# Latent attention with v stationary, P moving in two column halves of the array, and P divided by its sums while it is turned

## The chip, the cores and the metric

One core of one Trainium2 chip runs the whole program. The metric is the device time of one execution in microseconds (us); the median of three runs of the kernel before is 2729.82 us. PE is TensorE, PEld its loads of stationary operands ("weights"), DVE is VectorE, ACT is ScalarE, POOL is GpSimd, SP is SyncE.

## What is computed

Two sequences (512 and 256 tokens, 1024 features, all float32) go through two layers of a gated encoder with four branches and a convolutional feed-forward part. The change touches one branch, the latent attention with four heads. Its core, cut from the reference:

```python
q = rms_norm(q, g_qn); k = rms_norm(k, g_kn)      # heads of 64 + 32 (rope) values
q = q * (dqk ** -0.5)
def block(qi):                                     # 128 queries at a time
    s = jnp.einsum('bqhd,bkhd->bhqk', qi, k, preferred_element_type=jnp.float32)
    p = jax.nn.softmax(s, axis=-1)                 # over all keys of the sequence
    return jnp.einsum('bhqk,bkhd->bqhd', p.astype(v.dtype), v)   # v: 64 per head
...
return o @ w_o
```

The result of a 128-token tile is 128 tokens by 4 x 64 values. What follows (the product with `w_o`) wants it turned, with the 256 features on the partitions and split into a high and a low part.

## The kernel before

The code issues instructions in the order in which it calls them; each engine works through its own queue in that order, and waits between engines follow from the tiles. Two kinds of work are laced together. The large projections (`tm`, matmuls at L522, and `fm`, L498) run in a straight line, and after each step they call `q`, which advances a planned time `now` and then lets pending generators (`fast`, `slow`) issue their next piece when their planned time has come. Where the main line needs a generator's results it calls `drain`, which runs it to its end with nothing of the main line in between.

`mla` is such a generator. It starts under the projection of the first dilated group (`dil_proj(0)`); `self.drain(ed)` behind that projection then runs the rest of it alone. After the projections of latent q, k and v it has q and k turned per head (`qkT`, 96 partitions), and v as tokens by 256 features, 64 for each head. Then it makes a list of jobs, one for each tile of 128 queries and each head: 4 tiles x 4 heads with 4 key blocks (512 keys), then 2 tiles x 4 heads with 2 key blocks, 24 jobs a layer. A job is a tuple of steps:

- `score` (PE, L904): the 128 x S scores, S = 512 or 256, in a PSUM tile
- `low` (DVE, L909): the row minimum (the scores have their sign turned)
- `expo` (ACT, L915): the exponent into `P`, and in the same instruction the row sums, read out by an ACTIVATION_READ_ACCUMULATOR
- `turn` (PE, L921 calling `tr`, L511): each 128x128 block of P is transposed into PSUM; `tr` is TensorE's transpose, with the identity as second operand
- `copy` (DVE L930 for even heads, ACT L928 for odd ones): PSUM to `PT`
- `value` (PE, L937): for each key block a matmul with the turned P as stationary operand and the head's 64 columns of v moving; the four heads of a tile fill 256 columns of one PSUM tile `po`
- `done` (after the fourth head): DVE takes the reciprocals of the four sums (L944) and multiplies `po` by them into `mo` (L946); a generator put into `fast` then transposes `mo` in two blocks (`to_bin`, L511) and splits each into high and low (`split`: ACT L481, DVE L482).

`pipe` (L764) issues the steps of neighbouring jobs in turn. In its iteration i it calls, in three groups with a third of `w` planned time between them: score of job i and `done` of an earlier job; low of i and turn of i - 1; expo of i, copy of i - 1 and value of i - 2. PSUM tiles of this kind (`ps`) come from four buffers, SBUF tiles `s` (P, PT) from seven, small `st` tiles from eight. An f32 matmul is one instruction in the program and leaves two records in the trace (two weight loads, two passes); a transpose leaves one.

## Time and profile before

| | |
|---|---|
| runs | 2726.26, 2729.82, 2730.07 us; median 2729.82 |
| the profiled execution | 2730.13 us, span of its trace 2728.4 us |
| PE busy / PEld / DVE / ACT / POOL | 98% / 89% / 63% / 42% / 23% of the span |
| the chain that ended last | PE 86%, DVE 8%, issue 2%, ACT 2% |
| instructions of `value` (L937), both layers | 320 records, 42.2 us busy, loads 40.4 us |
| instructions of `score` (L904), both layers | 96 records, 44.8 us busy |

In the page a matmul's duration includes its way through the array, so busy times of pipelined matmuls overlap; what one costs is the distance between starts. In the timeline, neighbours of one line are merged (x8), and a bracket gives the engine's idle time ahead of the row and what ended it. PEclk is the share of TensorE's full clock that was granted (1.00 is 2.4 GHz, 0.50 is 1.2 GHz).

### The profile page before, as it was taken

To read this page: it belongs to the slowest core of one execution; us is meant where nothing else is said; L and a number is where in the kernel's file an instruction comes from. 1 tells how busy PE (TensorE), PEld (TensorE's weight loads), DVE (VectorE), ACT (ScalarE), POOL (GpSimd) and SP (SyncE) were. 2 spreads that over 40 slices of the span, in tenths; PEclk is the share of its full clock that TensorE was granted. 3 is DMA by queue.
4 is the path that set the end of the run, shared out by engine and by line. 5 is a ranking of instruction groups with operands and counts; after the bars stand their busy time and mean duration, and the time that the engine had idled before them with its cause. 6 is when DMAs were issued, how large, how long until landed. Compare 5 with 4: busy or idle time off the path is not lost.

```text
span 2728.4 us, 40139 instructions
## 1 busy us (share of the span) xinstructions
PE 2677.2 (98%) x15196; PEld 2439.2 (89%) x15196; DVE 1729.2 (63%) x3048; ACT 1141.3 (42%) x2333; POOL 634.0 (23%) x592
## 2 busy tenths in 40 slices
PE   9999999999998999999999999999999989999999
PEld 8779998888898899999987799988888989999998
DVE  6644448887437866686746454478873388766875
ACT  6443443223224554554544434432232255544553
POOL 3402123122222212222314021131121212222221
PEclk9999999999999999999999999999999999999999
DMA  5101113212232466646731111131212325567556
GB/s 167 43 28 37 41 56 114 63 62 62 62 129 81 107 148 128 155 121 147 193 94 43 28 40 48 51 114 63 66 59 62 132 74 127 137 130 161 125 136 163
DMA packets 143264, 258.87 MB, mean 95 GB/s; under 512 B 20192, under 2 KB 36192, under 8 KB 143072
## 3 DMA queue, kind: packets, MB, share of 16 engines
q1 hardware_dynamic: 118368, 197.59, 22.7%
q0 software_dynamic: 24704, 58.73, 12.4%
q8 instruction: 119, 1.95, 0.3%
q14 instruction: 73, 0.60, 0.1%
HBM read 205.78 MB, written 48.91 MB: 93 GB/s over the span
## 4 chain that ended last, share of the span: by engine, by line
PE 86%; DVE 8%; issue 2%; ACT 2%; POOL 1%; DMA 1%; SPq 0%; DVEq 0%; ACTq 0%; POOLq 0%
PE mm L498 35%; PE ps L498 26%; PE mm L522 16%; PE ps L511 3%; DVE wlo L453 2%; PE ps L904 1%; PE ps L1137 1%; PE ps L937 1%; PE ps L1088 1%; DMA raw<-wu 1%; PE ps L1140 1%; POOL st L529 1%; DVE b L612 1%; DVE hl L628 0%; PE ps L851 0%
## 5 line engine op out<-in xcount | busy, mean ns | idle before, releaser
L453 DVE TENSOR_TENSOR wlo<-raw,whi 128x512 fp32r<-128x512 f32 (+1 forms) x616 | 480.8, 790 | 142.3 <-ACT whi L444 117.9
L498 PE MATMUL ps<-b,whi 128*128 128x384 f32 (+2 forms) x1888 | 466.2, 340 | 17.3 <-ACT s L1532 11.7
L444 ACT CAST whi<-raw 128x512 fp32r<-128x512 f32 (+1 forms) x616 | 370.0, 614 | 237.2 <-PE ps L498 72.3
L498 PEld LDWEIGHTS ps<-b,whi 128*128 128x128 f32 x1888 | 329.7, 191 | 34.4 <-ACT s L1532 12.3
L498 PE MATMUL mm<-b,whi 128*128 128x512 f32 (+1 forms) x1504 | 322.9, 336 | 0.6 <-DVE b L1576 0.6
L522 PE MATMUL mm<-whi,hh 128*128 128x512 f32 (+2 forms) x752 | 308.8, 411 | 7.5 <-ACT hh L547 5.7
L498 PE MATMUL mm<-hh,whi 128*128 128x512 f32 (+1 forms) x1152 | 302.1, 343 | 0.0
L498 PE MATMUL ps<-b,wlo 128*128 128x384 f32 (+2 forms) x944 | 299.1, 339 | 0.0
L498 PE MATMUL mm<-hh,wlo 128*128 128x512 f32 (+1 forms) x1152 | 296.8, 338 | 0.0
L498 PE MATMUL mm<-hl,whi 128*128 128x512 f32 (+1 forms) x1152 | 294.7, 337 | 0.0
L522 PE MATMUL mm<-whi,hl 128*128 128x512 f32 (+2 forms) x752 | 278.8, 371 | 0.8 <-DVE hl L554 0.8
L522 PE MATMUL mm<-wlo,hh 128*128 128x512 f32 (+2 forms) x752 | 278.5, 370 | 0.0
L498 PE MATMUL ps<-hh,whi 128*128 128x384 f32 x768 | 259.6, 338 | 8.5 <-ACT whi L444 8.5
L498 PEld LDWEIGHTS mm<-b,whi 128*128 128x128 f32 x1504 | 237.0, 188 | 26.6 <-DVE b L1576 1.2
L498 PE MATMUL ps<-hl,whi 128*128 128x384 f32 x768 | 259.4, 338 | 1.2 <-DVE hl L628 1.2
L498 PE MATMUL ps<-hh,wlo 128*128 128x384 f32 x768 | 258.2, 336 | 0.0
L529 POOL TENSOR_TENSOR st<-st,mhalf 128x16 f32<-128x16 f32 (+5 forms) x50 | 95.0, 1900 | 573.6 <-DVE st L1012 355.7
L1368 POOL TENSOR_TENSOR b<-b,b 128x768 f32<-128x768 f32 x48 | 100.2, 2087 | 463.4 <-DVE b L1363 463.4
L498 PEld LDWEIGHTS mm<-hh,whi 128*128 128x128 f32 x1152 | 177.3, 189 | 26.6 <-issue 3.1
L522 PEld LDWEIGHTS mm<-whi,hh 128*128 128x128 f32 x752 | 177.6, 236 | 25.6 <-issue 10.2
L498 PEld LDWEIGHTS mm<-hl,whi 128*128 128x128 f32 x1152 | 175.7, 188 | 25.1
L498 PEld LDWEIGHTS mm<-hh,wlo 128*128 128x128 f32 x1152 | 176.0, 188 | 24.4
(233 smaller groups left out, 4607.9 us busy)
## 6 DMA issues: line engine op xcount, KB each, us to landing
raw<-wu SPq DMA_DIRECT2D x600, 256.0 KB, 2.7
xsp<-y POOLq DMA_DIRECT2D x66, 384.0 KB, 5.8
raw<-wu POOLq DMA_DIRECT2D x80, 256.0 KB, 4.9
b<-xsp SPq DMA_DIRECT2D x24, 384.0 KB, 6.8
xsp<-b POOLq DMA_DIRECT2D x22, 384.0 KB, 5.7
do<-ot SPq DMA_DIRECT2D x36, 132.0 KB, 1.8
b<-do SPq DMA_DIRECT2D x12, 384.0 KB, 3.5
raw<-wu SPq DMA_DIRECT2D x16, 208.0 KB, 3.6
```

The source lines that it names most:

```text
L444: self.nc.scalar.copy(hi, raw)
L453: self.nc.vector.tensor_sub(lo, raw, hi.bitcast(F32))
L498: nc.tensor.matmul(ap, w, x[:, c0:c1], start=(k == 0 and i == 0 and not more), stop=(k == K - 1 and i == 2), skip_group_check=more)
L511: self.nc.tensor.transpose(out, x, self.ident)
L522: nc.tensor.matmul(ap, x[:, cols], w, start=(k == 0 and i == 0), stop=(k == 7 and i == 2))
L529: self.nc.gpsimd.tensor_tensor(r, ms, self.mhalf[:, 0:n], op=ALU.pow)
L612: nc.vector.scalar_tensor_tensor(h, h, g[:, k:k + 1], self.rbc[:, cols], op0=ALU.mult, op1=ALU.mult)
L904: nc.tensor.matmul(sc[:, 0:S], qkT[hh][:, 128 * t:128 * t + 128], qkT[4 + hh][:, 128 * t0:128 * t0 + S], start=True, stop=True)
L937: nc.tensor.matmul(sh["po"][:, hh, :], PT[:, 128 * kb:128 * kb + 128], v[(t0 + kb) // 3][:, (t0 + kb) % 3, 64 * hh:64 * hh + 64], start=(k ...
L1088: nc.tensor.matmul(sc[:, x, y, 0:W], qT[y][rr, 128 * t:128 * t + 128], kT[y][rr, k0:k0 + W], start=True, stop=True)
L1137: nc.tensor.matmul(po[:, 0, 2 * y + par, :], PT[0:c - a, 2 * z + y, :], vv[:, hc], start=(z == 0), stop=(z == 1))
L1368: nc.gpsimd.tensor_add(a, a, t)
```

## The change

`turn` no longer calls the transpose. A new step `diag` takes the reciprocal of the head's sums, and multiplies the identity by it, row by row; `turn` is then an ordinary matmul with a block of P stationary and that diagonal moving, which turns the block and divides it at once. `value` has v stationary (128 keys x 64 features) and the turned P moving (128 queries); it is called for every head but acts for odd ones alone, and then for two heads, key block by key block in alternation. The even head's result goes to PSUM partitions 0 to 63, the odd one's to 64 to 127, so the two take different column halves of the array and `po` comes out with features on the partitions. `done` therefore has nothing to transpose or to multiply: it splits the two halves of `po`, in line and no longer from a generator. `pipe` calls `diag` (step 7) at the start of the iteration after `expo`, ahead of `done`; the condition on `len(jobs[j])` leaves the other attention, whose jobs have seven steps, as it was.

```diff
-            for group in (((0, 0), (6, 2)), ((1, 0), (3, 1)), ((2, 0), (4, 1), (5, 2))):
+            for group in (((0, 0), (7, 1), (6, 2)), ((1, 0), (3, 1)), ((2, 0), (4, 1), (5, 2))):
...
-                    if 0 <= j < n:
+                    if 0 <= j < n and f < len(jobs[j]):
...
         def expo():
             e["P"] = P = self.s(S)
-            if hh == 0:
-                sh["l"] = self.st(4)
-            nc.scalar.activation(P, e.pop("sc")[:, 0:S], AF.Exp, bias=e["mn"], scale=-1.0,
-                                 accum_out=sh["l"][:, hh:hh + 1])
+            e["l"] = self.st(1)
+            nc.scalar.activation(P, e.pop("sc")[:, 0:S], AF.Exp, bias=e["mn"], scale=-1.0, accum_out=e["l"])
+
+        def diag():
+            r = self.st(1)
+            nc.vector.reciprocal(r, e.pop("l"))
+            e["dg"] = dg = self.pm.tile([128, 128], F32, tag="mo", name=self.nm("mo"), bufs=2)
+            nc.vector.tensor_scalar_mul(dg, self.ident, r)
 
         def turn():
-            P = e.pop("P")
+
+            P, dg = e.pop("P"), e.pop("dg")
             e["pt"] = pt = self.ps()
             for kb in range(n):
-                self.tr(pt[:, 128 * kb:128 * kb + 128], P[:, 128 * kb:128 * kb + 128])
+                nc.tensor.matmul(pt[:, 128 * kb:128 * kb + 128], P[:, 128 * kb:128 * kb + 128], dg, start=True,
+                                 stop=True)
...
         def value():
-            if hh == 0:
-                sh["po"] = self.ps((128, 4, 64))
-            PT = e.pop("PT")
+
+            if hh % 2 == 0:
+                return
+            if hh == 1:
+                sh["po"] = self.ps((128, 2, 128))
+            PT = [sh.pop(hh - 1), sh.pop(hh)]
             for kb in range(n):
-                nc.tensor.matmul(sh["po"][:, hh, :], PT[:, 128 * kb:128 * kb + 128],
-                                 v[(t0 + kb) // 3][:, (t0 + kb) % 3, 64 * hh:64 * hh + 64], start=(kb == 0),
-                                 stop=(kb == n - 1))
+                for x in range(2):
+                    h = hh - 1 + x
+                    nc.tensor.matmul(sh["po"][64 * x:64 * x + 64, hh // 2, :],
+                                     v[(t0 + kb) // 3][:, (t0 + kb) % 3, 64 * h:64 * h + 64],
+                                     PT[x][:, 128 * kb:128 * kb + 128], start=(kb == 0), stop=(kb == n - 1),
+                                     skip_group_check=True)
 
         def done():
             if hh == 3:
-                r = self.st(4)
-                nc.vector.reciprocal(r, sh["l"])
-                mo = self.pm.tile([128, 256], F32, tag="mo", name=self.nm("mo"), bufs=2)
-                nc.vector.tensor_mul(mo.rearrange("p (h d) -> p h d", h=4), sh["po"],
-                                     r.unsqueeze(2).broadcast_to([128, 4, 64]))
-                sh.clear()
-                self.go_fast(self.late_bin(b, mo, t), 1.0)
+                po = sh.pop("po")
+                for f in range(2):
+                    self.split(b[f][0][:, 128 * t:128 * t + 128], b[f][1][:, 128 * t:128 * t + 128], po[:, f, :])
 
-        return score, low, expo, turn, copy, value, done
+        return score, low, expo, turn, copy, value, done, diag
```

How this moves instructions, at two places. First TensorE, in the first layer, where the attention runs alone on tiles of four key blocks. Rows give line, operation, output<-inputs and the moving size, and the engines waited for; L904 is a score, L511 a transpose of P (`s`) or of a finished tile (`mo`) with the identity (`hc`), L937 a value product with v (`b_815`, `b_816`). Before, for two heads:

```order
L904 MATMUL ps_1841<-b_1429,b_1381 128x512 [waits PE_49]
L511 MATMUL ps_1849<-hc,s_1833 128x128 [waits DVE_49,Activation_49]
L511 MATMUL ps_1849<-hc,s_1833 128x128 x3
L937 MATMUL ps_1858<-b_815,s_1835 128x64 x3
L937 MATMUL ps_1858<-b_816,s_1835 128x64
L511 MATMUL ps_1863<-hc,mo_1845 128x128 [waits DVE_49]
L511 MATMUL ps_1863<-hc,mo_1845 128x128
L904 MATMUL ps_1870<-b_1489,b_1457 128x512 [waits Activation_49]
L511 MATMUL ps_1874<-hc,s_1854 128x128 [waits Activation_49]
L511 MATMUL ps_1874<-hc,s_1854 128x128 x3
L937 MATMUL ps_1858<-b_815,s_1856 128x64 x3
L937 MATMUL ps_1858<-b_816,s_1856 128x64
```

Now, for two heads (L905 is the score, L928 the turn by the diagonal `mo`, L949 a value product; two alternating L949 rows of each v tile stand for all):

```order
L905 MATMUL ps_1877<-b_1429,b_1381 128x512 [waits PE_49]
L928 MATMUL ps_1889<-mo_1881,s_1864 128x128 [waits DVE_49,Activation_49]
L928 MATMUL ps_1889<-mo_1881,s_1864 128x128 x3
L905 MATMUL ps_1899<-b_1489,b_1457 128x512 [waits PE_49]
L928 MATMUL ps_1907<-mo_1903,s_1894 128x128 [waits DVE_49,PE_49,Activation_49]
L928 MATMUL ps_1907<-mo_1903,s_1894 128x128 x3
L949 MATMUL ps_1917<-s_1867,b_815 64x128
L949 MATMUL ps_1917<-s_1897,b_815 64x128 [waits Activation_49]
...
L949 MATMUL ps_1917<-s_1867,b_816 64x128
L949 MATMUL ps_1917<-s_1897,b_816 64x128
```

A value group used to stand between every turn and the next score; now one stands there after every second turn, and every turn waits for DVE too. The two transposes of a finished tile are gone from the queue.

Second VectorE at the same place. Before (L909 is a minimum, L930 a copy, L944 and L946 the reciprocals and the product of a finished tile, L482 its low parts):

```order
L930 COPY s_1835<-ps_1828 128x512 [waits PE_49]
L944 RECIPROCAL st_1843<-st_1715 128x4 [waits Activation_49]
L946 TENSOR_TENSOR mo_1845<-ps_1777,st_1843 128x256 [waits DVE_49,PE_49]
L909 TENSOR_REDUCE st_1847<-ps_1841 128x1 [waits PE_49]
L482 TENSOR_TENSOR b_1525<-ps_1863,b_1524 128x128 [waits Activation_49]
L482 TENSOR_TENSOR b_1527<-ps_1863,b_1526 128x128 [waits Activation_49]
L909 TENSOR_REDUCE st_1872<-ps_1870 128x1 [waits PE_49]
```

Now (L919 and L921 are `diag`, L910 the minimum, L937 the copy, L482 the low parts):

```order
L937 COPY s_1867<-ps_1859 128x512 [waits PE_49]
L919 RECIPROCAL st_1879<-st_1865 128x1 [waits Activation_49]
L921 TENSOR_SCALAR mo_1881<-hc,st_1879 128x128 [waits DVE_49]
L482 TENSOR_TENSOR b_1525<-ps_1824,b_1524 128x128 [waits Activation_49]
L482 TENSOR_TENSOR b_1527<-ps_1824,b_1526 128x128 [waits Activation_49]
L910 TENSOR_REDUCE st_1887<-ps_1877 128x1 [waits PE_49]
L919 RECIPROCAL st_1901<-st_1895 128x1 [waits Activation_49]
L921 TENSOR_SCALAR mo_1903<-hc,st_1901 128x128 [waits DVE_49]
L910 TENSOR_REDUCE st_1905<-ps_1899 128x1 [waits PE_49]
```

Every head now has a reciprocal and a 128x128 product ahead of the next head's minimum, and the low parts of a finished tile have moved from behind that minimum to ahead of it.

## Rows read from the trace of the kernel before

**Rows 1.** The page: busy time by engine, and the chain by engine.

```profile
PE 2677.2 (98%) x15196; PEld 2439.2 (89%) x15196; DVE 1729.2 (63%) x3048; ACT 1141.3 (42%) x2333; POOL 634.0 (23%) x592
...
PE 86%; DVE 8%; issue 2%; ACT 2%; POOL 1%; DMA 1%; SPq 0%; DVEq 0%; ACTq 0%; POOLq 0%
```

**Rows 2.** Windows of layer 1: length, busy by engine (instructions), PEclk, DMA share, GB/s.

```profile
137.90:160.30 22.40, 22.40 (x162) 19.51 (x161) 10.42 (x19) 10.04 (x25) 5.02 (x9) 1.00 0.10 32
160.30:189.50 29.20, 28.33 (x186) 21.83 (x185) 15.35 (x33) 14.47 (x40) 0.00 (x0) 1.00 0.12 33
189.50:200.90 11.40, 9.48 (x61) 7.46 (x60) 5.15 (x17) 5.42 (x20) 0.00 (x0) 0.95 0.07 18
200.90:207.00 6.10, 6.10 (x18) 4.96 (x18) 1.61 (x4) 0.53 (x2) 0.00 (x0) 0.54 0.01 3
```

**Rows 3.** The same windows of layer 2, its last two.

```profile
1551.20:1562.60 11.40, 9.35 (x61) 7.37 (x60) 5.12 (x17) 5.42 (x20) 0.00 (x0) 0.96 0.08 18
1562.60:1568.60 6.00, 6.00 (x24) 5.21 (x25) 1.61 (x4) 0.54 (x2) 0.00 (x0) 0.80 0.00 0
```

**Rows 4.** Timeline, one head of four blocks: start, length, engine, line, operation.

```profile
168.74 1.08 PE L904 MATMUL ps<-b,b 96*128 96x512 f32 x2
...
169.65 0.60 PE L511 MATMUL ps<-hc,s 128*128 128x128 f32 x4
...
169.85 0.69 DVE L909 TENSOR_REDUCE st<-ps 128x1 f32<-128x512 f32 x1 [1.50 <-PE ps L904]
169.98 0.97 PEld L937 LDWEIGHTS ps<-b,s 128*128 128x128 f32 x8
...
170.58 0.69 ACT L915 ACTIVATE s<-ps,st 128x512 f32<-128x512 f32 x1 [0.88 <-DVE st L909]
...
171.06 0.17 DVE L944 RECIPROCAL st<-st 128x4 f32<-128x4 f32 x1
171.17 0.19 ACT L915 ACTIVATION_READ_ACCUMULATOR s<-ps,st 128x1 f32 x1
171.33 0.42 DVE L946 TENSOR_TENSOR mo<-ps,st 128x256 f32<-128x256 f32 x1
171.42 0.14 PEld L511 LDWEIGHTS ps<-hc,s 128*128 128x128 f32 x1 [0.24 <-ACT s L915]
...
179.34 0.97 PEld L937 LDWEIGHTS ps<-b,s 128*128 128x128 f32 x8
```

**Rows 5.** Timeline, heads of two blocks, all engines.

```profile
189.51 0.52 PEld L937 LDWEIGHTS ps<-b,s 128*128 128x128 f32 x4
...
193.71 0.65 PE L904 MATMUL ps<-b,b 96*128 96x256 f32 x2
...
194.20 0.38 PE L511 MATMUL ps<-hc,s 128*128 128x128 f32 x2
...
195.23 0.19 ACT L915 ACTIVATION_READ_ACCUMULATOR s<-ps,st 128x1 f32 x1
...
195.65 0.53 PEld L937 LDWEIGHTS ps<-b,s 128*128 128x128 f32 x4
```

**Rows 6.** Timeline, PE, an f32 product of 128x128 operands in the gating unit.

```profile
410.87 1.05 PE L1336 MATMUL ps<-b,b 128*128 128x128 f32 x8
```

**Rows 7.** Timeline, PE then PEld: scores split by rows between plain matmuls.

```profile
298.06 0.40 PE L522 MATMUL mm<-wlo,hh 128*128 128x512 f32 x1
298.29 0.40 PE L522 MATMUL mm<-whi,hl 128*128 128x512 f32 x1
298.62 1.16 PE L1088 MATMUL ps<-b,b 64*128 64x128 f32 x16
...
300.17 0.40 PE L522 MATMUL mm<-wlo,hh 128*128 128x512 f32 x1
...
298.61 0.97 PEld L1088 LDWEIGHTS ps<-b,b 64*128 64x128 f32 x16 [0.25 <-issue]
299.71 0.31 PEld L522 LDWEIGHTS mm<-whi,hh 128*128 128x128 f32 x1
```

**Rows 8.** One line's instructions: count, shortest/median/longest ns, first and last start.

```profile
L704 DVE TENSOR_SCALAR s<-hc,rt x12: 274/280/746, 43.0 to 1383.2; 128x128 f32<-128x128 f32 x12
```

More of the change, by code (lines that the diff above doesn't have):

```diff
@@ L912, in expo @@
             e["P"] = P = self.s(S)
-            if hh == 0:
-                sh["l"] = self.st(4)
-            nc.scalar.activation(P, e.pop("sc")[:, 0:S], AF.Exp, bias=e["mn"], scale=-1.0,
-                                 accum_out=sh["l"][:, hh:hh + 1])
+            e["l"] = self.st(1)
[5 more added lines that the diff above has]
+            nc.vector.tensor_scalar_mul(dg, self.ident, r)
         def turn():
-            P = e.pop("P")
+            P, dg = e.pop("P"), e.pop("dg")
             e["pt"] = pt = self.ps()
             for kb in range(n):
-                self.tr(pt[:, 128 * kb:128 * kb + 128], P[:, 128 * kb:128 * kb + 128])
+                nc.tensor.matmul(pt[:, 128 * kb:128 * kb + 128], P[:, 128 * kb:128 * kb + 128], dg, start=True,
+                                 stop=True)
         def copy():
-            e["PT"] = PT = self.s(S)
+            sh[hh] = PT = self.s(S)
             pt = e.pop("pt")
```

## The prediction

> **What bounds the kernel now.** I read the page first: TensorE (PE) is busy 98% of the span and 86% of the chain that ended last is PE [rows 1]. So the edit is worth what it does to TensorE's own time, plus every stop of TensorE that it makes or removes. Next the windows around the edited attention of the first layer [rows 2]. It has three parts: three heads run between the projection matmuls of L522 (137.9 to 160.3, PE full), then thirteen heads of four key blocks alone (160.3 to 189.5), then eight heads of two blocks alone (189.5 to 200.9, PE 9.48 of 11.40). The second layer repeats this to about a tenth [rows 2, 3], so every sum below is made for one layer and doubled. "Alone" is what matters: in these 40.6 us no other work can fill a stop.
>
> Then the timeline of one head of four blocks [rows 4]. Score is two passes; its first starts at 168.74 and the turn's first at 169.65: **0.91**. A pass of weights is loaded every (0.97 - 0.19) / 7 = 0.111, so the value group's eight take 8 x 0.111 = **0.89**, and the four transposes, one pass each, 0.44 ((0.60 - 0.27) / 3 = 0.11 a pass). These add to 2.24, and four heads take 179.34 - 169.98 = **9.36**, 2.34 each. TensorE paces itself here. For two blocks score is 194.20 - 193.71 = 0.49, but four heads take 195.65 - 189.51 = **6.14**, 1.53 each, against 0.49 + 0.22 + 0.45 = 1.16 of PE work [rows 5]: there the chain through the other engines already shows.
>
> **The change part by part.**
> *Turn.* A transpose is one pass. The new product with the diagonal is an ordinary f32 matmul, and such a matmul leaves two passes in this trace: the existing 128x128 product has eight records for four matmuls, one per (1.05 - 0.275) / 7 = 0.111 [rows 6]. So turn goes from 0.44 to 0.89 for four blocks and from 0.22 to 0.45 for two. That is certain.
> *Value.* Before, two heads cost 2 x 0.89 = 1.78. Now there are as many passes, but of 64 columns, two heads side by side. The trace has no such split by columns; the nearest row splits by rows of the array: sixteen passes 128 wide have their weights loaded in 0.97, so they go two at a time, eight steps of 0.111 = 0.89 [rows 7]. Bounds for a pair of four-block heads: 0.89 (side by side) and 1.78 (one by one); I take 0.89, since that row is the same 64-of-128 split.
> *Changing the split.* In [rows 7] the plain matmuls start every 0.235, so the next was due at 298.29 + 0.235 = 298.52. The split group's first load is at 298.61 and its first step 0.111 later, 298.72: 0.20 lost. It streams until 298.72 + 0.89 = 299.61; the next plain load is at 299.71, and that matmul's start, one spacing before 300.17, is 299.94: 0.33 lost. Together 0.53 for each value group, between 0 and 0.53 if columns were milder; I take 0.53. The group for two heads is then 1.42 with four blocks (before 1.78) and 0.45 + 0.53 = 0.98 with two (before 0.90).
> *The diagonal.* This is a new link: exponent, reciprocal, product with the identity, turn. From the score's end at 169.65 the exponent and its sum are done at 171.17 + 0.19 = 171.36, so 1.71 [rows 4]. To this come one hand-over of 0.04 (170.54 to 170.58), 0.27 (171.06 to 171.33, reciprocal until the DVE instruction that reads it starts), 0.28 for a 128x128 TENSOR_SCALAR [rows 8], 0.06 to the first load (171.36 to 171.42) and 0.11 for that load: **2.47** until the turn can run. What covers it on PE is decided by the order: without a value group between, the turn of the head before and the next score, 0.89 + 0.91 = 1.80. So in every second head TensorE stands **0.67**. Where the value group lies between, the cover is 0.67 + 0.89 + 1.42 + 0.91 and nothing waits. With two blocks the chain is 195.23 + 0.19 - 194.20 = 1.22 [rows 5] plus the same 0.76, so 1.98, over 0.45 + 0.49 = 0.94: **1.04** of waiting. Behind the waiting turn stand, in order, the value group and the next score; DVE's next minimum and ACT's next exponent then wait for that score.
> *Removed:* the two transposes of each finished tile and its product with the reciprocals; the cycles of before contain them, the new sums don't. The two splits of a tile remain and now stand on DVE ahead of the next minimum; their cover is the score then running, and without it at most 0.3 a tile is lost.
>
> **Sum.** Four heads of four blocks: 4 x 0.91 + 4 x 0.89 + 2 x 1.42 + 2 x 0.67 = 11.38, +2.02 over 9.36; thirteen heads: 3.25 x 2.02 = +6.6. Four heads of two blocks: 4 x 0.49 + 4 x 0.45 + 2 x 0.98 + 2 x 1.04 = 7.80, +1.66 over 6.14; eight heads: +3.3. The three heads under the projection see PE work alone, the waits being filled: 3 x 0.45 of turns less one pair's 0.36: +1.0. One layer +10.9, both +21.8. The profiled execution took 2730.13 (span 2728.4), 0.3 above the median of the runs, so 2730.1 + 21.8 = 2751.9, and for the median **2751**.
>
> **The clock.** Granted 1.00 through the heads of four blocks, the clock stands at 0.95 in the last stretch and 0.54 (mostly 1.2 instead of 2.4 GHz) for 6 us behind it [rows 2]; in layer 2 at 0.96 and 0.80 [rows 3]. At the lower level half the time is lost, so these cost about 0.6 + 2.8 + 0.5 + 1.2 = 5. My sum leaves them as they are. The Trainium skill, "TensorE: Matmul & The Clock Gate", section on PE-mode transpose, says that transposes don't count as TensorE activity the way matmuls do. By it matmuls instead of transposes would keep the clock up and give back up to 5, so 2746; the trace neither shows nor refutes it, since the full level was granted through 29 us with transposes in them.
>
> **The rivals.**
> A. *The column halves don't run side by side.* Against it the row split of [rows 7]; for it that no row shows columns. Then a pair costs 1.78 + 0.53 and 0.90 + 0.53: + 8 x 0.89 + 4 x 0.45 = 8.9 a layer, **2769**. The same page, section on packing small matmuls, states that weights load beside running matmuls only when their row groups differ, which column halves' don't. By that rule this rival is the likelier one; but whole-array loads here already follow every 0.111 while the passes before them, over the same rows, still run [rows 4], which speaks against it.
> B. *Changing to columns is free.* Then 0.53 goes from 24 groups, -12.7: **2739**.
> C. *No wait for the diagonal*, because TensorE is late by other things: 6.5 x 0.67 + 4 x 1.04 = 8.5 a layer less, **2735**, just about the same as now.
> D. *Faster: the value groups nearly vanish.* Place: the twelve groups of a layer, which I priced at 8 x 1.42 + 4 x 0.98 = 15.3. A layer comes out 10.9 dearer with them, so the two kernels meet when the groups cost 15.3 - 10.9 = 4.4 a layer, 29% of my price; below that the changed one is faster, at nothing at all by 4.4 a layer: **2721**. It would need all passes of a group to share one stream and no loss on entering. No row goes that far.
> E. *The other half isn't done*: the diagonal leaves the transposes one-pass. The order shows plain MATMULs with two operands, so no.
>
> **How the numbers follow.** Two runs of this kernel can be told apart from about 0.2%, 5.5 us. Chances: forecast, 2740 to 2764, 0.61; A, with anything above 2764, 0.17; B, 0.09; C or a mixture that stays within 0.2%, 0.08; D, 0.05. The range runs from B's side to A's: 2736 to 2770, which leaves out D, most of C and costs above A, about 0.17. Faster 0.05, same 0.08, slower 0.87.
>
> **What would show it.** Value groups: 8 steps in about 0.9 with idle weight loading before and after (right), or 1.8 (A). The first load of every second turn ended by DVE's TENSOR_SCALAR, with 0.5 to 0.8 idle (right); ended by the score before it (C). A cycle of four heads near 11.4 and 7.8; DVE and ACT no busier than half. The rest of the program should keep its time to a microsecond or two apart from the clock's drops; if the sum of both attention stretches doesn't carry the difference, the prediction is wrong in its place, whatever the total.

## The result, and the profile after

| | before | after |
|---|---|---|
| median of the runs, us | 2729.57 | 2741.57 (2741.10 to 2743.58) |
| ratio, 95% interval | | 1.0051 [1.0038, 1.0064] |
| the profiled execution, and its span | 2730.13, 2728.4 | 2743.58, 2741.8 |

The changed kernel is slower by half a per cent, 12.0 us by the medians and 13.4 by the two profiled executions. The forecast was 2751 with a range from 2736 to 2770: right in its sign and range, 9 us too high. (The median of before is of the three runs above and one more.) The page of after, with the two rows that answer to [rows 1]:

```profile
PE 2680.7 (98%) x15332; PEld 2436.8 (89%) x15332; DVE 1742.9 (64%) x3120; ACT 1142.9 (42%) x2333; POOL 633.1 (23%) x592
...
PE 84%; DVE 10%; issue 2%; ACT 2%; POOL 1%; DMA 1%; SPq 0%; DVEq 0%; ACTq 0%; POOLq 0%
```

The share of PE hardly moves, but in the chain two points have gone from PE to DVE: somewhere TensorE now waits for VectorE. The windows show where. I take the stretch of each layer in which the attention runs alone, from the last projection matmul (L522) ahead of it to the first behind it. Columns: length; then busy time (instructions) of PE, PEld, DVE, ACT, POOL; PEclk, DMA share, GB/s. Before:

```profile
160.00:201.00 41.00, 38.20 (x249) 29.69 (x247) 20.66 (x50) 20.00 (x60) 0.00 (x0) 0.98 0.11 31
1521.60:1562.60 41.00, 38.08 (x248) 29.60 (x248) 20.73 (x50) 20.00 (x60) 0.00 (x0) 0.99 0.13 33
```

After:

```profile
160.00:209.20 49.20, 41.77 (x311) 29.67 (x309) 26.57 (x78) 20.75 (x61) 0.00 (x0) 0.97 0.11 28
1528.90:1577.00 48.10, 40.63 (x310) 28.86 (x308) 26.55 (x78) 20.81 (x61) 0.00 (x0) 1.00 0.11 28
```

The stretch grows by 8.2 and 7.1 us. PE is busy 3.6 and 2.6 longer, and idle 49.20 - 41.77 = 7.4 and 48.10 - 40.63 = 7.5, where it was idle 2.8 and 2.9: **some 3 us more work and 4.6 us more waiting a layer**. About 1 us of layer 1's 8.2 is the clock, which stands at half for 3 us at the end of this stretch and stood so for 1.3 before. In layer 2 it is the other way round: 1.0 us at half before, none after, so a little of what the change costs there is hidden.

One head of four blocks, in the timeline of after, answering to [rows 4] (start, length, engine, line; the bracket is idle time ahead and what ended it):

```profile
166.55 0.85 PEld L949 LDWEIGHTS ps<-s,b 128*64 128x64 f32 x16
...
170.34 0.16 DVE L919 RECIPROCAL st<-st 128x1 f32<-128x1 f32 x1 [0.90 <-ACT s L915]
170.53 0.29 DVE L921 TENSOR_SCALAR mo<-hc,st 128x128 f32<-128x128 f32 x1
...
170.94 0.97 PEld L928 LDWEIGHTS ps<-mo,s 128*128 128x128 f32 x8 [1.31 <-ACT s L935]
170.97 1.13 PE L928 MATMUL ps<-mo,s 128*128 128x128 f32 x8 [0.51 <-DVE mo L921]
...
172.03 0.85 PEld L949 LDWEIGHTS ps<-s,b 128*64 128x64 f32 x16
...
173.05 0.30 PEld L905 LDWEIGHTS ps<-b,b 96*128 96x128 f32 x2 [0.17 <-issue]
...
177.57 0.85 PEld L949 LDWEIGHTS ps<-s,b 128*64 128x64 f32 x16
```

The turn (L928) waits for the diagonal, and TensorE stands idle until L921 releases it. (The bracket of the loads at 170.94 names the copy L935, which ended at almost the same time; e4 below shows a turn that starts while that copy still runs, so the copy is not what the turn needs.) Then sixteen value loads take 0.85, two at a time. The next group of this kind starts at 177.57, and the one before at 166.55; a group stands for two heads, so four heads take **11.02** (forecast 11.38, before 9.36).

Heads of two blocks, TensorE alone, answering to [rows 5]:

```profile
197.34 0.66 PE L949 MATMUL ps<-s,b 128*64 128x128 f32 x8
...
200.42 0.68 PE L928 MATMUL ps<-mo,s 128*128 128x128 f32 x4 [0.89 <-DVE mo L921]
201.03 0.66 PE L949 MATMUL ps<-s,b 128*64 128x128 f32 x8
...
204.60 0.68 PE L928 MATMUL ps<-mo,s 128*128 128x128 f32 x4 [1.39 <-DVE mo L921]
205.22 0.66 PE L949 MATMUL ps<-s,b 128*64 128x128 f32 x8
```

Four of them take 205.22 - 197.34 = **7.88** (forecast 7.80, before 6.14), with two stops for L921, the longer where the splits of a finished tile stand on DVE ahead of the next minimum.

### The profile page after: what moved, and what is told of

It is laid out like the page before. It is cut to its first block, busy times and chain, and to the rows that moved or that the text cites. A ratio compares the mean times of both kernels' runs of the same rounds, so it can differ in the third digit from the quotient of the medians.

```text
span 2741.8 us, 40525 instructions
## 1 busy us (share of the span) xinstructions
PE 2680.7 (98%) x15332; PEld 2436.8 (89%) x15332; DVE 1742.9 (64%) x3120; ACT 1142.9 (42%) x2333; POOL 633.1 (23%) x592
## 3 DMA queue, kind: packets, MB, share of 16 engines
q0 software_dynamic: 24704, 58.73, 12.5%
## 4 chain that ended last, share of the span: by engine, by line
PE 84%; DVE 10%; issue 2%; ACT 2%; POOL 1%; DMA 1%; SPq 0%; DVEq 0%; ACTq 0%; POOLq 0%
PE mm L498 35%; PE ps L498 26%; PE mm L522 15%; DVE wlo L453 2%; PE ps L511 2%; PE ps L928 1%; PE ps L1146 1%; PE ps L1097 1%; PE ps L949 1%; POOL st L529 1%; PE ps L1149 1%; PE ps L905 1%; DVE s L1464 1%; DVE b L612 1%; DVE hl L628 0%
## 5 line engine op out<-in xcount | busy, mean ns | idle before, releaser
L522 PE MATMUL mm<-whi,hh 128*128 128x512 f32 (+2 forms) x752 | 307.4, 409 | 8.0 <-ACT hh L547 6.1
L522 PE MATMUL mm<-whi,hl 128*128 128x512 f32 (+2 forms) x752 | 278.0, 370 | 0.1
L522 PE MATMUL mm<-wlo,hh 128*128 128x512 f32 (+2 forms) x752 | 277.6, 369 | 0.0
L522 PEld LDWEIGHTS mm<-whi,hh 128*128 128x128 f32 x752 | 177.4, 236 | 26.6 <-issue 11.0
```

Of the source, the lines that this page charges most:

```text
L522: nc.tensor.matmul(ap, x[:, cols], w, start=(k == 0 and i == 0), stop=(k == 7 and i == 2))
```

## The experiments

The theory: half of the loss is TensorE waiting for the diagonal in every second head, the other half work on TensorE, the second pass of the turn above all and then the change of the split; the column halves themselves do run side by side. The rivals: that it is all work, so that a covered wait wins nothing; and that the column halves cost what the change costs. Two kernels take the change apart, three work on the wait, one on the halves, three look for a better version, and two are controls.

The ratio is to the runs of before beside which each kernel ran (medians 2727.44 to 2729.57). "Alone" is the stretch above, layer 1 / layer 2, "idle" PE's idle time in it, "four" and "two" the time of four heads of four and of two blocks (in e3 the last value groups start in parts, so "two" can't be read there). The rows were not all run side by side, and the medians of before differ by 2 us, so a difference of 2 us between two rows says nothing.

| kernel | us | ratio | alone | idle | four | two |
|---|---|---|---|---|---|---|
| before | 2729.57 | 1 | 41.0 / 41.0 | 2.8 / 2.9 | 9.36 | 6.14 |
| after | 2741.57 | 1.0051 [1.0038, 1.0064] | 49.2 / 48.1 | 7.4 / 7.5 | 11.02 | 7.88 |
| e1 diagonal alone | 2750.69 | 1.0081 [1.0069, 1.0094] | 51.3 / 51.3 | 5.7 / 5.7 | 11.92 | 8.12 |
| e2 value alone | 2716.32 | 0.9955 [0.9942, 0.9967] | 38.5 / 38.5 | 5.4 / 5.4 | 8.85 | 6.16 |
| e3 turn later | 2728.41 | 1.0003 [0.9994, 1.0012] | 42.9 / 42.9 | 1.9 / 1.9 | 9.62 | |
| e4 diagonal ready | 2729.02 | 1.0004 [0.9994, 1.0013] | 42.4 / 42.4 | 2.0 / 2.0 | 9.86 | 6.70 |
| e5 half after half | 2748.51 | 1.0076 [1.0063, 1.0088] | 52.4 / 51.5 | 6.6 / 7.3 | 11.99 | 8.57 |
| e9 diagonal twice | 2752.95 | 1.0087 [1.0074, 1.0101] | 52.1 / 52.8 | 10.7 / 8.5 | 11.67 | 8.67 |
| e6 P divided | 2727.59 | 0.9997 [0.9988, 1.0006] | 43.6 / 43.0 | 7.2 / 7.4 | 9.59 | 6.21 |
| e7 and ACT copies | 2726.08 | 0.9988 [0.9979, 0.9997] | 42.6 / 43.8 | 6.6 / 6.4 | 9.51 | 6.15 |
| e10 and minimum first | 2719.74 | 0.9972 [0.9963, 0.9981] | 38.8 / 39.5 | 5.4 / 5.2 | 8.60 | 6.07 |
| e11 e3, minimum first | 2727.70 | 1.0004 [0.9995, 1.0013] | 43.1 / 43.1 | 2.3 / 2.3 | 9.59 | 6.30 |
| e15 before, turn later | 2726.36 | 0.9998 [0.9989, 1.0007] | 41.6 / 41.7 | 2.4 / 2.4 | 9.36 | 5.84 |

### The change in two halves

e1, against before (`value` untouched, a finished tile copied where it was multiplied):

```diff
-                self.tr(pt[:, 128 * kb:128 * kb + 128], P[:, 128 * kb:128 * kb + 128])
+                nc.tensor.matmul(pt[:, 128 * kb:128 * kb + 128], P[:, 128 * kb:128 * kb + 128], dg, start=True,
+                                 stop=True)
...
-                nc.vector.tensor_mul(mo.rearrange("p (h d) -> p h d", h=4), sh["po"],
-                                     r.unsqueeze(2).broadcast_to([128, 4, 64]))
+                nc.vector.tensor_copy(mo.rearrange("p (h d) -> p h d", h=4), sh["po"])
```

> The kernel before with one half of the change alone: P is divided while it is turned (reciprocal, product with the identity, two-pass matmul in place of the transpose), the value product stays as it was, and a finished tile is copied where it was multiplied by the reciprocals. Theory (the second pass of a turn costs TensorE time, and the turn waits for the diagonal where nothing covers it): with four key blocks a value group stands in every head, so turn, value and score cover 0.89 + 0.89 + 0.91 = 2.69 of a chain of 2.47, no wait, and four heads take about 11.5 (before 9.36); with two blocks the cover is 0.45 + 0.45 + 0.49 = 1.39 of 1.98, 0.59 of waiting in every head, and four heads take about 8.1 (before 6.14). A layer 6.9 + 4 + about 1 for the heads under the projection, 2752 to 2755 in all: slower than both kernels. Rival (the value half, with its change of the split and its order, is what costs): about the time of before, below 2737.

Measured 2750.69, a little under the range of the theory and far from the rival. TensorE's rows of e1 (L926 the turn, L942 the value, L904 the score):

```profile
179.99 1.13 PE L926 MATMUL ps<-mo,s 128*128 128x128 f32 x8 [0.93 <-DVE mo L920]
180.95 1.00 PE L942 MATMUL ps<-b,s 128*128 128x64 f32 x8
181.79 1.08 PE L904 MATMUL ps<-b,b 96*128 96x512 f32 x2
182.71 1.06 PE L926 MATMUL ps<-mo,s 128*128 128x128 f32 x8
183.60 1.00 PE L942 MATMUL ps<-b,s 128*128 128x64 f32 x8
```

From value to value it is 2.65, without a wait, as the cover of 2.69 said; once a tile the turn waits 0.93, which I had not counted (the splits of the finished tile stand on VectorE ahead of the diagonal there), so four heads take 11.92 and not 11.5. With two blocks 8.12, as expected. The diagonal alone costs more than the whole change, so the rival falls.

e2, against after:

```diff
         def diag():
-            r = self.st(1)
-            nc.vector.reciprocal(r, e.pop("l"))
-            e["dg"] = dg = self.pm.tile([128, 128], F32, tag="mo", name=self.nm("mo"), bufs=2)
-            nc.vector.tensor_scalar_mul(dg, self.ident, r)
+            e.pop("l")
...
-                nc.tensor.matmul(pt[:, 128 * kb:128 * kb + 128], P[:, 128 * kb:128 * kb + 128], dg, start=True,
-                                 stop=True)
+                self.tr(pt[:, 128 * kb:128 * kb + 128], P[:, 128 * kb:128 * kb + 128])
```

> The other half alone: v stationary and two heads in column halves, as in the changed kernel, but P is turned by one-pass transposes and no diagonal is made; the division of P by its sums is left out altogether. Theory: a pair of heads with four blocks costs two scores, two turns of 0.44 and one value group of 1.22 to 1.42, 3.9 to 4.2 where TensorE paces, against 4.68 before; but every second head has no value group to cover the way from score over minimum and exponent to the turn (1.7 against 1.35), some 0.4 of waiting a pair, so 4.4; with two blocks 2.8 to 2.9 against 3.07. Some 2.5 a layer less than before: about 2724, faster than both kernels. Rival (the column halves and their change of split are what the change costs): 2735 to 2742.

Measured 2716.32, better than expected. TensorE's weight loads of e2 (L945 the value, L511 the second turn of a pair):

```profile
163.94 0.85 PEld L945 LDWEIGHTS ps<-s,b 128*64 128x64 f32 x16 [0.17 <-issue]
...
167.74 0.42 PEld L511 LDWEIGHTS ps<-hc,s 128*128 128x128 f32 x4 [1.18 <-ACT s L915]
168.32 0.85 PEld L945 LDWEIGHTS ps<-s,b 128*64 128x64 f32 x16 [0.17 <-issue]
...
172.79 0.20 PEld L945 LDWEIGHTS ps<-s,b 128*64 128x64 f32 x4 [0.17 <-issue]
```

Four heads of four blocks take 172.79 - 163.94 = 8.85, as expected (twice 4.4): in every pair the second turn still waits, here for ScalarE's exponent. The value half by itself is a gain of 11.6, the diagonal half a loss of 22.7; their sum, -11.6 + 22.7 = +11.1, is near the change's +12.0. The traces say the same where the attention runs (the projection with the first three heads and the alone stretch, both layers): 25.6 more in e1, 7.8 less in e2, 17.4 more in after, all against before. Part of e2's gain is work left out, and how the rest is shared between the column halves and the two transposes a tile that fall away was not tried.

### The wait

e3, against after; turn, copy, value and done come one iteration later:

```diff
+        for i in range(n + 4):
+            for group in (((0, 0), (7, 1), (6, 4)), ((1, 0), (3, 2)), ((2, 0), (4, 2), (5, 3))):
```

> The changed kernel with all its work, but turn, copy, value and done of a head are issued one iteration later, so that another head's score and turn stand on TensorE between the exponent and the turn that needs it. Nothing is left out. Theory (TensorE stands 0.7 in every second head of four blocks and about 1.0 in every second head of two, or more, because the diagonal isn't ready): these waits go, 6.5 x 0.7 + 4 x 1.0 = 8.5 a layer, four heads of four blocks 11.0 down to about 9.7, of two 7.9 to about 5.9: 2724 to 2728, faster than before. Rival (the cost is work on TensorE, the second pass of the turn and the switching, and a wait removed is only moved to another place): 2739 to 2742, as the changed kernel.

Measured 2728.41: 13.2 won back, just above the range of the theory, and level with before where the theory had it faster. TensorE's rows of e3 (L916 the score, L939 the turn, L960 the value):

```profile
172.62 1.09 PE L960 MATMUL ps<-s,b 128*64 128x128 f32 x16
173.64 1.12 PE L916 MATMUL ps<-b,b 96*128 96x512 f32 x2
174.60 1.05 PE L939 MATMUL ps<-mo,s 128*128 128x128 f32 x8
175.50 1.02 PE L916 MATMUL ps<-b,b 96*128 96x512 f32 x2
176.36 1.05 PE L939 MATMUL ps<-mo,s 128*128 128x128 f32 x8
```

No row has a bracket: in this pair nothing waits, and the idle time of PE in the alone stretch falls from 7.4 to 1.9, less than before's. The pair from 172.62 to the next value group at 177.34 is 4.73 of work alone (the other pair of the cycle takes 4.89; there the loads of the second turn wait for ScalarE's exponent). In it the turn takes 175.50 - 174.60 = 0.90 and the score 176.36 - 175.50 = 0.86, so the value group with its switching is 4.73 - 2 x 0.90 - 2 x 0.86 = **1.21**. Against two such pairs the changed kernel's four heads hold (11.02 - 2 x 4.73) / 2 = **0.78** of waiting in every second head. The end of the stretch, where the last turns and values have nothing beside them, gets longer by the extra iteration. Not all of the 13.2 is the wait that the change brought: idle time falls below before's, and the projection with the first three heads takes 75.2 in each layer, against 76.7 in after and 75.7 before.

e4, against after; the identity stands for the diagonal:

```diff
-            r = self.st(1)
-            nc.vector.reciprocal(r, e.pop("l"))
-            e["dg"] = dg = self.pm.tile([128, 128], F32, tag="mo", name=self.nm("mo"), bufs=2)
-            nc.vector.tensor_scalar_mul(dg, self.ident, r)
+            e.pop("l")
+            e["dg"] = self.ident
```

> The changed kernel with the identity in place of each head's diagonal: the turn is the same two-pass matmul, in the same order, but there is no reciprocal and no product to wait for; the division of P by its sums is left out. Theory (reciprocal and product, 0.76 with their hand-overs, are the end of the chain that TensorE waits for): with four blocks the wait falls from 0.7 to 0.0 to 0.1, with two blocks from about 1.0 to 0.3 to 0.4; 6.5 x 0.65 + 4 x 0.65 = 6.8 a layer, about 2728, and the turn then waits for ACT's exponent. Rival (the cost is the work on TensorE): 2739 to 2742.

Measured 2729.02, as the theory said: 12.5 less, 6.8 and 5.7 of it in the two stretches. TensorE's rows of e4 (L926 the turn), first of four blocks, then of two:

```profile
174.88 1.16 PE L926 MATMUL ps<-hc,s 128*128 128x128 f32 x8
...
199.47 0.71 PE L926 MATMUL ps<-hc,s 128*128 128x128 f32 x4 [0.79 <-ACT s L915]
```

With four blocks the idle 0.51 ahead of the turn is gone (9.86 for four heads, of which e3's work is 9.46), and the turn at 174.88 starts beside ScalarE's copy (174.73 to 175.31); with two the turn still stands, but now for ScalarE's exponent, and the cycle has lost 1.18. So what after waits for is reciprocal and product: e4 makes them needless, e3 covers them, and the result is the same.

e9, against after; the product is made twice:

```diff
             nc.vector.tensor_scalar_mul(dg, self.ident, r)
+            nc.vector.tensor_scalar_mul(dg, self.ident, r)
```

> The changed kernel with the diagonal's product made twice, one after the other, into the same tile: 0.2 to 0.28 more between the exponent and the turn, for VectorE work alone. Theory (the turn of every second head waits for exactly this chain): each wait grows by 0.2 to 0.28; 6 to 6.5 pairs of four blocks and 4 of two, 10.5 a layer, 4 to 6 in all: 2745.5 to 2747.5. Rival (the wait is for something else, or TensorE's own work sets the pace): 2740 to 2743.

Measured 2752.95, 11.4 more instead of 4 to 6. VectorE's rows of e9:

```profile
178.98 0.29 DVE L921 TENSOR_SCALAR mo<-hc,st 128x128 f32<-128x128 f32 x1
179.30 0.29 DVE L922 TENSOR_SCALAR mo<-hc,st 128x128 f32<-128x128 f32 x1
```

From product to product it is 0.32, not 0.2 to 0.28, and a pair of four blocks grows by (11.67 - 11.02) / 2 = 0.33: the wait takes the added time in full. By that 6.5 x 0.33 + 4 x 0.40 = 3.7 a layer, 7.5 in all; the two stretches grew by 2.9 and 4.7 (how this splits between the layers is blurred by the clock, which stands at half for 3 us in the first stretch of after and for 6.8 in the second of e9). The two profiled executions differ by 2752.03 - 2743.58 = 8.5, so nearly all of it lies in these stretches; the rest of the 11.4 lies between executions.

### The column halves

e5, against after:

```diff
-            for kb in range(n):
-                for x in range(2):
+            for x in range(2):
+                for kb in range(n):
```

> The changed kernel with one loop turned round: in a value group all key blocks of the even head come first, then all of the odd head, so neighbouring matmuls use the same column half. Same instructions, same result. Theory (neighbours in different halves share a step because TensorE takes passes in order and only the next one can join; then the two heads are one by one): the group goes from eight steps to sixteen with four blocks and from four to eight with two, 0.89 and 0.44 more for each of 8 and 4 groups, 8.9 a layer, 2757 to 2760. Rival (each half of the array works through its own passes, whatever the order): 2740 to 2743. Second rival (the pairing is not what the group's length comes from, 64 columns being short of themselves): also 2740 to 2743, but then each half's loads follow each other every 0.05 or so instead of two every 0.11.

Measured 2748.51, between theory and rival, and neither was right. The loads of a value group in e5, against 0.85 in after:

```profile
175.07 1.34 PEld L949 LDWEIGHTS ps<-s,b 128*64 128x64 f32 x16
```

The single records of the trace tell how: the even head's eight matmuls start from 175.07 on, after the first at steps of 0.109, and a second series of eight, with the same steps, starts at 175.563, while the first series has 175.666, 175.776 and 175.885 still to come. The load at 175.561 carries the wait for ScalarE's copy, which only the odd head's first has; it started with two loads of the even head (175.668 and 175.777) not yet made, though they stand ahead of it in the program. So **each half works through its own passes, at its own 0.109**, and the second half began 0.49 late, behind six of the first half's loads; why then is not shown. So TensorE does not start everything in the order of its queue here. The second rival falls too: one half's loads come every 0.109, not every 0.05. The pair then costs 0.48 more (5.99 against 5.51), and with two blocks 0.35. Interleaving the heads key block by key block, as the change does, is the right order.

The Trainium skill, "TensorE: Matmul & The Clock Gate", section on packing small matmuls, says that loads overlap running matmuls only where the row groups differ, and that matmuls start in program order. This trace disagrees with both for column halves, which share all rows: the load at 175.561 runs beside the even head's matmul from 175.557 to 175.830 (that end is modelled), and the odd head's first matmul (175.563) starts ahead of the even head's sixth (175.666).

### Towards a better version

The value half won and the two-pass turn lost. e6 keeps the one and avoids the other: P is divided on VectorE, in place, and turned by one-pass transposes; the order is e3's.

```diff
-            nc.vector.tensor_scalar_mul(dg, self.ident, r)
+            nc.vector.tensor_scalar_mul(e["P"], e["P"], r)
```

> A version with the whole computation: value as in the changed kernel (two heads in column halves), but P is divided on VectorE, in place, 128 x S by its reciprocals, and then turned by one-pass transposes; turn, copy, value and done come one iteration later, as in the run with the later turn. Theory (what was gained is the value half, 4.82 to about 3.9 a pair with four blocks if nothing waits, and the longer chain is covered by the extra head): VectorE has two minima (0.69), two reciprocals (0.17), two products of 128x512 (estimated 0.5 to 0.7 from 0.28 for a quarter of the width), one copy (0.69) and the splits in a pair, 3.8 to 4.2, so it or TensorE sets 3.9 to 4.2; with two blocks 2.2 to 2.5 a pair: 5 to 8 a layer less than the run with the later turn, 2712 to 2719. Rival (VectorE becomes the bound and the wait moves there): 2722 to 2730.

> As the run with P divided on VectorE, but all copies of the turned P are ScalarE's, so VectorE has 0.69 less in a pair and ScalarE about as much more (3.0 to 3.3 of 3.9). Theory (with VectorE relieved TensorE alone sets the pace, 3.9 a pair): 0 to 2 a layer less than with the copies shared, 2710 to 2716. Rival (ScalarE, or the way through it, becomes the bound): 2718 to 2725.

(e7 is e6 with `nc.scalar.copy(PT, pt[:, 0:S])` for every head.) Measured 2727.59 and 2726.08: e6 falls in the range of its rival, e7 above both of its ranges, and neither gains what was expected. VectorE's rows of e6, then ScalarE's:

```profile
176.00 0.16 DVE L930 RECIPROCAL st<-st 128x1 f32<-128x1 f32 x1 [0.31 <-ACT s L926]
176.20 0.49 DVE L931 TENSOR_SCALAR s<-s,st 128x512 f32<-128x512 f32 x1
176.60 0.68 DVE L921 TENSOR_REDUCE st<-ps 128x1 f32<-128x512 f32 x1
178.19 0.17 DVE L930 RECIPROCAL st<-st 128x1 f32<-128x1 f32 x1 [0.91 <-ACT s L926]
```

```profile
177.38 0.69 ACT L926 ACTIVATE s<-ps,st 128x512 f32<-128x512 f32 x1 [1.41 <-DVE st L921]
177.97 0.19 ACT L926 ACTIVATION_READ_ACCUMULATOR s<-ps,st 128x1 f32 x1
```

VectorE isn't full (busy 28.05 of 43.6 us in the alone stretch of layer 1, and idle 0.91 ahead of the reciprocal), yet it sets the pace by its order: the minimum of the next head stands behind this head's product, which waits for this head's exponent, which waited for its minimum. From one reciprocal to the next that round takes 178.19 - 176.00 = 2.19 and not less, whatever TensorE does; with the 0.82 that the splits of a finished tile add, four heads take 9.59. Giving the copies to ScalarE (e7) leaves the round as it is. e10 breaks it, against e7:

```diff
-            for group in (((0, 0), (7, 1), (6, 4)), ((1, 0), (3, 2)), ((2, 0), (4, 2), (5, 3))):
+            for group in (((0, 0), (6, 4)), ((1, 0), (7, 1), (3, 2)), ((4, 2), (2, 0), (5, 3))):
```

> The run with P divided on VectorE and all copies on ScalarE, with the order on two queues changed: VectorE takes the minimum of the next head ahead of the reciprocal and product of this one, and ScalarE copies a turned P ahead of the next exponent. The whole computation is made. Theory (that run went at 2.4 a head, 9.6 for four heads, because the minimum stood on VectorE behind a product that waits for the exponent before it, so minimum, exponent, reciprocal and product, 0.69 + 0.88 + 0.16 + 0.49 and hand-overs, followed each other round and round): the round is broken, TensorE sets the pace, two scores, two turns of 0.44 and a value group of 1.22, 3.9 a pair of four blocks in place of 4.8 and about 2.3 for two blocks in place of 3.1; 6 to 7 a layer less, 2711 to 2716. Rival (the engines are simply full, or TensorE waits for the copies): 2722 to 2728.

Measured 2719.74, between theory and rival, and faster than both kernels: 0.9972 [0.9963, 0.9981] of before, some 22 below the changed one. VectorE's rows of e10:

```profile
176.41 0.69 DVE L921 TENSOR_REDUCE st<-ps 128x1 f32<-128x512 f32 x1 [1.70 <-PE ps L916]
177.02 0.15 DVE L930 RECIPROCAL st<-st 128x1 f32<-128x1 f32 x1
177.21 0.49 DVE L931 TENSOR_SCALAR s<-s,st 128x512 f32<-128x512 f32 x1
```

And the value groups of e10 that are four heads apart, and a second turn (L511):

```profile
174.22 0.85 PEld L955 LDWEIGHTS ps<-s,b 128*64 128x64 f32 x16 [0.17 <-issue]
182.82 0.20 PEld L955 LDWEIGHTS ps<-s,b 128*64 128x64 f32 x4 [0.17 <-issue]
```

```profile
177.84 0.63 PE L511 MATMUL ps<-hc,s 128*128 128x128 f32 x4 [0.17 <-DVE s L931]
```

Now the minimum waits for TensorE's score and the reciprocal for nobody: the round is broken. Four heads take 182.82 - 174.22 = 8.60, still 0.8 more than the 7.8 estimated for TensorE's work alone: the second turn of a pair waits for VectorE's product (0.17 in one pair of this cycle, 0.84 in the other), and TensorE is idle 5.3 a layer. The edit changes the order on two engines, and what each is worth was not tried.

Two controls. e11 is e3 with the order of e10:

> The run with the later turn of the changed kernel (diagonals and two-pass turns, everything computed), with the same new order on VectorE and ScalarE: minimum ahead of the diagonal, copy ahead of the exponent. Theory: with four blocks TensorE paces it already (9.62 for four heads, its own work), so nothing moves there; with two blocks the round of minimum, exponent and diagonal (about 1.8 of 1.47 a head by now) goes, 0.5 to 1 a layer: 2726 to 2728. Rival (the order costs something, as the exponent comes later): 2729 to 2732.

Measured 2727.70, as e3. With four blocks 9.59 as expected, since TensorE paces there. With two blocks I had expected a gain, and there is none (the alone stretch is 43.1 against 42.9); that the total falls in the theory's range is luck, since e3's time lies right beside that range. e15 is before with turn, copy, value and done one iteration later, nothing else:

> The kernel before, nothing of the change, with turn, copy, value and done one iteration later: what the later turn is worth without the change. Theory: with four blocks TensorE paces the kernel before (9.36 of work for four heads), so nothing is won; with two blocks 6.14 fall towards TensorE's 4.7, 2 to 3 a layer, less about 1 for the longer end: 2723 to 2727. Rival (the waits with two blocks are not the turn's): 2728 to 2730. If it comes out below the changed kernel with the later turn (2728.4), the change is worth nothing even with its waits covered.

Measured 2726.36, no different from before: 9.36 for four blocks, unchanged, and 5.84 for two, given back by the longer end. So before had next to no wait that a later turn covers at a profit, and the change with its waits covered (e3, 2728.41) is at best level with it.

## Why the prediction was right, and where it was off

**Turn, two passes.** Forecast 0.89, measured 0.90 in e3; e1 and e2 show this half to be the costly one. Right.

**Column halves side by side (rival A).** Right: 0.85 for sixteen loads, 1.21 for the group with its switching, where rival A wanted 2.3. The step from a row split [rows 7] to a column split held; e5 shows each half at its own passes.

**Changing the split. This term was mis-sized: 0.53 forecast, 0.34 measured.** The same reading, now in a place that [rows 7] stood for, under the projection in after (PE):

```profile
152.01 0.28 PE L522 MATMUL mm<-whi,hl 128*128 128x256 f32 x1
152.22 1.09 PE L949 MATMUL ps<-s,b 128*64 128x128 f32 x16
153.24 0.38 PE L522 MATMUL mm<-whi,hh 128*128 128x256 f32 x1
153.47 0.28 PE L522 MATMUL mm<-wlo,hh 128*128 128x256 f32 x1
```

The plain matmuls come every 0.12, so the next was due at 152.13; the first step lies one short load (0.05, from the first load of a half to its second) behind 152.22, 0.14 lost. Eight steps of 0.109 end at 153.14; the next plain one starts one spacing before 153.47, at 153.35: 0.20 lost. The row split had cost 0.53 beside matmuls of 512 columns. In the heads of four blocks the group came out the same, 1.21 in e3, 0.34 over its 0.87. So four heads take 4 x 0.86 + 4 x 0.90 + 2 x 1.21 + 2 x 0.78 = 11.02 where the forecast had 11.38: the switching gives 2 x 0.21 less, the score 4 x 0.05 less, the turn 0.04 more, and the wait 2 x 0.11 more. That is 0.36 x 3.25 = 1.2 a layer of the difference. (The sum closes by construction: the wait was read as what is left of 11.02 beside e3's work.)

**Waiting for the diagonal (rival C).** Four blocks: forecast 0.67, measured 0.78, released by the instruction named in advance. Of the 0.11, 0.04 is the cover, 0.90 + 0.86 instead of 1.80. Two blocks: forecast 1.04; measured (7.88 - 4 x 0.49 - 4 x 0.45 - 2 x 0.79) / 2 = 1.27, because the splits of a finished tile stand ahead of the next minimum, which I had priced at 0.3 a tile at most. That was a term that the sum left out. There the smaller switching and the longer wait cancel by luck, and 7.80 against 7.88 looks better than it was. VectorE was busy 54% of the alone stretch, a little over the half that the prediction named.

**Heads between cycles.** I multiplied by 13 / 4. From the group of the fourth head to that of the sixteenth before took 187.96 - 160.32 = 27.64 and after 192.72 - 161.01 = 31.71: +4.07, where three cycles make 3 x 1.66 = 4.98. The last pair of four blocks is followed by the short scores of two blocks and takes 4.12 instead of 5.5; before, the same end was 3 x 9.36 - 27.64 = 0.44 shorter than three cycles, after 3 x 11.02 - 31.71 = 1.35. That is the other 0.9.

**Under the projection.** Forecast +1.0 a layer; the projection that holds the first three heads (its L522 matmuls, from the first to the last ahead of the alone stretch) went from 75.7 to 76.7 in both layers. Right.

**The sum.** Forecast +10.9 a layer; measured 8.2 + 1.0 and 7.1 + 1.0, so +17.3 for both, where the forecast had 21.8. The remaining 3.9 down to 13.4 lies outside the change, more than the microsecond or two that the prediction allowed the rest of the program: four long stretches without this attention (the start, the two behind it in layer 1, the one behind it in layer 2) came out 0.7 to 1.2 shorter each. It can't be put to this change. Everything but the projection with the first three heads and the alone stretch took 2494.6 in the profiled execution of before, 2490.7 in after, and 2486.6 to 2490.9 in the other eleven kernels, 2488.7 in e15, which has nothing of the change. Some of it is the clock (behind layer 1's attention after stands 1.8 us less at half); for the rest the cause stays open. So the mechanism was right and its size, 21.8 for 17.3, was off by the switching and by the heads between cycles. The total alone would not have told it: 2741.57 lies nearer to rival B's 2739 than to the forecast, and it is the 0.34 lost at each value group that speaks against B.

**The clock.** I left it as it was, and in total it was: at half the full clock TensorE spent 58.0 us in thirteen stretches before, and 58.0 in twelve after (the closing microseconds left out). The stretch behind the attention of layer 1 is still there after the change:

```profile
206.10:212.90 6.80, 6.51 (x21) 4.95 (x22) 1.32 (x4) 0.90 (x3) 0.00 (x0) 0.50 0.01 2
```

That of layer 2 [rows 3] is gone, and one elsewhere is longer instead. The Trainium skill, "TensorE: Matmul & The Clock Gate", section on PE-mode transpose, says that transposes don't count as TensorE's activity the way matmuls do, so plain matmuls in their place would have kept the clock up. No run here shows it: e2, which keeps the transposes, spent 54.6 us at the lower level, and e3, which has the product, 54.6 as well; all kernels lie between 41.0 and 61.4 in no such order.

Rivals B, D and E fall with this: switching is not free, the value groups did not vanish (the price of a layer's twelve was 15.3, measured 8 x 1.21 + 4 x 0.79 = 12.8), and the turn has its two passes.

## What to carry to other kernels

Halving the time of one TensorE step by packing two heads into it wins less than that time: the same step was the cover for the chain through the other engines. Without a new link in that chain the packing still won here (e2, with the division left out, and e10); with one (0.76 of reciprocal, product and hand-overs) the link shows in every head that lost its cover. Before putting arithmetic into a transpose, count the passes: here an ordinary f32 matmul took two where a transpose took one. And when an engine that is idle a third of the time still sets the pace, look for a round in its queue: an instruction for the next head issued behind one that waits for this head.

## What the runs showed of the hardware that was not expected

- Each column half works through its own passes: one of 128 columns every 0.109 us, both halves at once, and one half's loads and matmuls overtake earlier ones of the other half (e5: 175.563 ahead of 175.666).
- Going from the whole array to column halves and back cost 0.34 us here, less than the 0.53 of the row split in [rows 7]; the shorter first load and the shorter plain matmuls are among the differences, and which of them matters was not tried.
- Dividing a 128x512 tile of P on VectorE took 0.49 us from SBUF to SBUF, where the minimum over the same width from PSUM took 0.68.
